# The second product of a squared-ReLU MLP by a Strassen 2x2 scheme, on one core

## Chip, core and metric

The kernel runs on one core of a Trainium2 chip. The metric is the device time of one execution in microseconds (us). TensorE does matrix products, VectorE and GpSimd elementwise work, ScalarE activations and casts, SyncE issues DMAs. In the profile they are PE (PEld is its weight load), DVE, POOL, ACT and SP.

## What is computed

One decoder block over 512 tokens with a stream of 1024 channels, in float32: a pre-norm, two token mixers side by side (latent attention and a gated convolution), a gated merge, then an MLP. Only the MLP is touched here:

```python
D_MODEL = 1024; SEQ = 512; D_FF = 4 * D_MODEL
def squared_relu_mlp(h, w_ff1, w_ff2):
    return jnp.square(jax.nn.relu(h @ w_ff1)) @ w_ff2
x = x + rms_norm(squared_relu_mlp(rms_norm(x, norm_mlp_pre), w_ff1, w_ff2), norm_mlp_post)
```

The second product is [512 x 4096] times [4096 x 1024].

## The kernel before

Float32 products are made of three matmuls on operands that are split into a rounded high half and a low half (function `mm3`, lines 86 to 88): high times high, high times low, low times high. A split is two instructions: ACT casts the source to the high half (line 91 for activations, 111 for weights), then DVE or POOL subtracts (lines 92 and 112). A matmul's moving side has up to 512 columns, its stationary side is 128 x 128.

Weights come through `wsplit` (lines 98 to 121): a 128 x 512 piece is loaded by an SP DMA into one of 6 buffers (tag `raw`), and split into one of 4 buffers each for the high (`whi`) and low (`wlo`) half.

The MLP has two stages. FF1 (lines 691 to 728) makes 32 feature blocks j of 128 features; a block is 24 matmuls, its weights in two pieces, and `ff1_end` squares the positive part into `f1[j // 2][:, j % 2, :]` (128 features x 512 tokens). Then FF2 contracts the 32 blocks. For each j two pieces of `w_ff2[j]` (128 features x 512 columns each) are loaded and split, `ff2_lhs(j)` splits the block's activations, and 4 token tiles x 2 column halves x 3 = 24 matmuls accumulate into all 8 PSUM banks (tiles `po`, one bank for 128 tokens x 512 columns). All 768 matmuls of FF2 have 512 moving columns. The low halves are made on DVE here (`eng=dve`). The last TAIL = 2 blocks are taken token tile by token tile (lines 751 to 765), so that the post-norm of one tile (`square_sums`, an ACT square with a running sum and two tiny POOL instructions, then `finish`: DVE and the store) runs beside the next tile's matmuls.

The order on each engine is set by the framework that builds the program: it takes the operations as written, may bring an operation forward on its engine while it waits for nothing there, and puts in the semaphore waits. Each engine then works strictly through its own list, SP's list of DMAs too.

Of the kernel before, what the change touches and what calls it, by code (L numbers as in the profile page):

```python
# [19 lines left out]
P = 128  # L20
# [38 lines left out]
def decoder_block(ctx: ExitStack, tc: tile.TileContext, a: dict, out: bass.AP):  # L59
# [24 lines left out]
    def mm3(o, lh, ll, rh, rl, first, last):  # L84
        """o += (lh + ll)^T (rh + rl) without the product of the two low parts (below float32's last bit)"""
        pe.matmul(o, lhsT=lh, rhs=rh, start=first, stop=False)  # L86
        pe.matmul(o, lhsT=lh, rhs=rl, start=False, stop=False)  # L87
        return pe.matmul(o, lhsT=ll, rhs=rh, start=False, stop=last)  # L88
# [10 lines left out]
    def wsplit(src, name, sizes=(512, 512), dst=None, eng=None):  # L99
        """load columns of src in pieces, split each; returns the piece (hi, lo) that holds a column range"""  # L100
# [75 lines left out]
    def rotary():  # L176
        """rotary tables: rows repeat every 32 partitions, sin carries the sign of its half"""
# [17 lines left out]
    # the tensor engine's clock rises while it works: products that nothing reads, until the first data are there  # L195
# [4 lines left out]
    # ---- first columns of W_in (latents, shared rope key), token rows; the pre-norm's scale of a token is  # L200
    # applied to its row of the product ----
    sp.dma_start(vecs, a["vecs"])
    xT = []
    with ExitStack() as s1:
# [10 lines left out]
        # squares of the stream, behind the splits that the first products wait for  # L215
# [29 lines left out]
        def latents(t):  # L245
            """norms of the latents of token tile t; shared rope key, twice"""
# [17 lines left out]
        def latents_t(t, c):  # L264
            """normalised latents to feature rows"""
# [9 lines left out]
        def token_scales():  # L275
            """rstd of the tokens, by partition and along the rows"""
# [94 lines left out]
    def rope(z, name):  # L371
        """rotary embedding of two stacked heads (rows of 64), fp32"""
# [29 lines left out]
    att, vts, sts, qks, pms, pTs = [], {}, {}, {}, {}, {}  # L402
    with ExitStack() as s3:
        r2 = open_pool(s3, "r2")

        def project_pair(pr):
            """values (token rows) and rotary queries of a pair of heads"""
# [16 lines left out]
            # hi and lo of one head stacked over the rows  # L424
# [7 lines left out]
        def project(h):  # L432
            """scaled queries and keys of a head without the rotary part, feature rows, split"""
# [112 lines left out]
    # causal depthwise convolution; running channel sum for the layer norm  # L546
# [29 lines left out]
    # layer norm over channels (partitions); sums over them through the tensor engine  # L576
# [37 lines left out]
    # pointwise projection, gated merge  # L614
# [21 lines left out]
    # output projection, post-norm, residual, MLP pre-norm  # L636
# [6 lines left out]
    def square_sums(src, name, jk=None):  # L643
        """rsqrt of the mean square of two halves, plus eps"""
# [68 lines left out]
    def ff2_lhs(j):  # L713
        fh, fl = stile(f"fh{j}", F32R), stile(f"fl{j}", F32R)
        split_psum(fh, fl, f1[j // 2][:, j % 2, :])
        return fh, fl

    for j in range(NF):
        if j == NF - 2:
            first = ff2_lhs(0)  # L720
# [9 lines left out]
    order = [tps] + [scs] * 2 + [cvtile] * 2 + [ps] * 3  # L730
    po = [[order[2 * t + hf](f"po{t}{hf}") for hf in range(2)] for t in range(NT)]
    ops = []
    for j in range(NF):
        w = wsplit(a["w_ff2"][j], f"f2{j}", eng=dve)
        fh, fl = ff2_lhs(j) if j else first
        ops.append((w, fh, fl))
        if j < NF - TAIL:
            for t in range(NT):
                sl = slice(t * P, (t + 1) * P)
                for hf in range(2):  # L740
                    mm3(po[t][hf], fh[:, sl], fl[:, sl], *w(hf * 512, 512), j == 0, False)

    def finish(t, o_, r):
# [7 lines left out]
    for t in range(NT):  # L751
        sl = slice(t * P, (t + 1) * P)
        o_ = wtile(f"o{t}")
        for hf in range(2):
# [3 lines left out]
            if hf == 0 and prev:  # L758
                finish(*prev)
# [66 lines left out]
```

## Time and profile before

| | |
|---|---|
| three runs | 842.81, 844.35, 845.77 us; median 844.35 us |
| profiled execution | span 842.8 us from the first to the last instruction |
| busy share of the span | PE 98%, PEld 81%, DVE 62%, ACT 45%, POOL 25% |
| FF1, from 496 us | 160.9 us to 656.9 us |
| FF2 | 656.9 to 835.9 us, then 6.9 us to the end |

The profile gives one execution. "Busy" counts an engine's instructions from start to end; an instruction that is held up by something the profile does not show still counts as busy, so a long record of an operation that is elsewhere short is a held one. Where two rows of one engine overlap a little, the distance from start to start is what an instruction costs in a row of them.

### The profile page before, as it was taken

Reading aid. Unit: us, or ns where it says so; the run is one execution under the profiler, and the core shown is the slowest. Engines: PE = TensorE matmul, PEld = TensorE weight load, DVE = VectorE, ACT = ScalarE, POOL = GpSimd, SP = SyncE. Lnnn points to the kernel's source line nnn. Section 1 sums busy time; section 2 is a strip of 40 time slices with the busy share of each in tenths; the row PEclk is TensorE's granted clock in tenths of the full one; section 3 lists DMA queues with packets and bytes.
Section 4 is the critical chain, followed back from the end, with each engine's and each line's share of the span. In section 5 each row is a group of like instructions: output and inputs, shape, how many; then the busy total and the mean of one; then the engine's idle time right before and its main releaser. Section 6 shows DMA issues by size and latency. Waiting matters only on the chain. (4 is left out here: it accounts for less than half of the span.)

```text
span 842.8 us, 10881 instructions
## 1 busy us (share of the span) xinstructions
PE 824.0 (98%) x3882; PEld 683.4 (81%) x3882; DVE 518.8 (62%) x838; ACT 377.0 (45%) x724; POOL 210.1 (25%) x201
## 2 busy tenths in 40 slices
PE   8989999999999999899999999999999999999996
PEld 8977888887878887687778898888888888888885
DVE  5689999999999986595554533333333333333335
ACT  7567775767572224365343333332333323332333
POOL 4244433434445446548611100000000000000001
PEclk9999999999999999899999999999999999999999
DMA  8412121222113324246440113232323232223312
GB/s 258 137 40 89 51 79 51 64 66 81 63 63 101 94 95 128 69 149 204 162 151 1 51 51 101 88 100 89 99 94 94 88 100 91 88 98 100 96 54 100
DMA packets 45126, 79.57 MB, mean 94 GB/s; under 512 B 5264, under 2 KB 10256, under 8 KB 45072
## 3 DMA queue, kind: packets, MB, share of 16 engines
q1 hardware_dynamic: 44640, 77.30, 29.0%
q0 software_dynamic: 432, 1.57, 0.5%
q8 instruction: 30, 0.49, 0.2%
q14 instruction: 24, 0.20, 0.1%
HBM read 76.76 MB, written 2.10 MB: 94 GB/s over the span
## 5 line engine op out<-in xcount | busy, mean ns | idle before, releaser
L112 DVE TENSOR_TENSOR wlo_f<-raw_f,whi_f 128x512 fp32r<-128x512 f32 x124 | 85.5, 690 | 213.3 <-ACT whi_f L111 213.1
L111 ACT CAST whi_f<-raw_f 128x512 fp32r<-128x512 f32 x124 | 76.6, 619 | 227.7 <-PE po L88 116.5
L559 DVE SCALAR_TENSOR_TENSOR cv<-u,convw,cv 128x512 f32<-128x512 f32 x232 | 161.8, 746 | 0.2
L87 PE MATMUL po<-wlo_f,fh 128*128 128x512 f32 x256 | 101.1, 395 | 0.0
L86 PE MATMUL po<-whi_f,fh 128*128 128x512 f32 x256 | 101.0, 395 | 0.0
L88 PE MATMUL po<-whi_f,fl 128*128 128x512 f32 x256 | 101.0, 395 | 0.0
L88 PE MATMUL pf<-h2h,wlo_f 128*128 128x512 f32 (+1 forms) x256 | 97.4, 381 | 0.0
L87 PE MATMUL pf<-h2l,whi_f 128*128 128x512 f32 (+1 forms) x256 | 97.4, 381 | 0.0
L86 PE MATMUL pf<-h2h,whi_f 128*128 128x512 f32 (+1 forms) x256 | 97.4, 380 | 0.0
L649 POOL TENSOR_SCALAR v_o<-ss_o 128x1 f32<-128x1 f32 x4 | 1.2, 302 | 351.5 <-ACT jo L647 351.5
L87 PEld LDWEIGHTS po<-wlo_f,fh 128*128 128x128 f32 x256 | 48.2, 188 | 11.4 <-DVE wlo_f L112 0.2
L88 PEld LDWEIGHTS po<-whi_f,fl 128*128 128x128 f32 x256 | 48.2, 188 | 11.3
L86 PEld LDWEIGHTS po<-whi_f,fh 128*128 128x128 f32 x256 | 48.2, 188 | 11.2
L112 POOL TENSOR_TENSOR wlo_gt<-raw_gt,whi_gt 128x512 fp32r<-128x512 f32 x32 | 43.9, 1374 | 50.5 <-ACT whi_gt L111 50.5
L88 PEld LDWEIGHTS pf<-h2h,wlo_f 128*128 128x128 f32 x256 | 48.2, 188 | 9.9
L87 PEld LDWEIGHTS pf<-h2l,whi_f 128*128 128x128 f32 x256 | 48.2, 188 | 9.9
L86 PEld LDWEIGHTS pf<-h2h,whi_f 128*128 128x128 f32 x256 | 48.3, 188 | 9.8
L86 PE MATMUL pg<-hTh,whi_gt 128*128 128x512 f32 x128 | 51.8, 405 | 0.0
L88 PE MATMUL pg<-hTh,wlo_gt 128*128 128x512 f32 x128 | 50.6, 395 | 0.0
L87 PE MATMUL pg<-hTl,whi_gt 128*128 128x512 f32 x128 | 50.6, 395 | 0.0
L111 ACT CAST whi_gt<-raw_gt 128x512 fp32r<-128x512 f32 x32 | 19.8, 618 | 41.3 <-PE pg L87 38.2
L86 PEld LDWEIGHTS pg<-hTh,whi_gt 128*128 128x128 f32 x128 | 24.6, 192 | 5.6 <-issue 0.5
(274 smaller groups left out, 1884.1 us busy)
## 6 DMA issues: line engine op xcount, KB each, us to landing
raw_f<-in_w_ff SPq DMA_DIRECT2D x128, 256.0 KB, 2.8
raw_gt<-in_w_zm SPq DMA_DIRECT2D x32, 256.0 KB, 2.6
raw_gb<-in_w_zm SPq DMA_DIRECT2D x16, 256.0 KB, 2.7
raw_ga<-in_w_zm SPq DMA_DIRECT2D x16, 256.0 KB, 2.6
raw_wo<-in_w_o SPq DMA_DIRECT2D x16, 256.0 KB, 2.7
raw_pw<-in_w_pw SPq DMA_DIRECT2D x16, 256.0 KB, 2.9
raw_wout<-in_w_out SPq DMA_DIRECT2D x16, 256.0 KB, 3.0
xT<-in_x_t SPq DMA_DIRECT2D x8, 256.0 KB, 4.2
```

The lines of the kernel that those rows point to most:

```text
L86: pe.matmul(o, lhsT=lh, rhs=rh, start=first, stop=False)
L87: pe.matmul(o, lhsT=lh, rhs=rl, start=False, stop=False)
L88: return pe.matmul(o, lhsT=ll, rhs=rh, start=False, stop=last)
L111: recent[act] = act.copy(hi, raw)
L112: recent[e] = e.tensor_tensor(lo, raw, f32(hi), ALU.subtract)
L559: dve.scalar_tensor_tensor(co[j] if tap == CW - 1 else acc[j], src, convw[:, i, tap:tap + 1], acc[j], ALU.mult, ALU.add)
L649: pool.tensor_scalar(v, ss[:, 0:1], ss[:, 1:2], EPS, ALU.add, ALU.add)
```

## The change

Let a pair p be the blocks 2p and 2p + 1 (NP = 16 pairs). The activations of a pair are a 2 x 2 matrix of quarters (feature block x half of the tokens), its weights one of (feature block x half of the columns), and the output one of (half of the tokens x half of the columns). The change computes the quarters of the output by a Strassen scheme with seven quarter products in place of eight. A quarter product is 2 token tiles x 3 matmuls of 512 columns. Three of the seven are made in a first sweep over the pairs (banks `ab` and `p2`), four in a second one (`ab` again and `cd`), since PSUM has 8 banks. Between the sweeps the first sums are copied out (lines 804 to 809); after the second the quarters are put together from them on DVE and POOL (lines 836 to 846), and the post-norm works from SBUF instead of PSUM.

Quarters are combined before they are split. The combinations run on POOL: in the first sweep one of weights (line 767, 128 x 512) and one of activations (line 765, 128 x 256), with two in-place updates of the activations (lines 777 and 778, 128 x 256); in the second one more update (line 784, 128 x 256) and three of weights (lines 786 to 788, 128 x 512). Splits are ACT casts (line 744) and DVE subtractions (line 745): in the first sweep four of 512 elements per partition and one of 256 for a pair, in the second one of 1024 and four of 512. Combinations of weights take buffers of tag `wlo`; the split weights lie in the 4 tiles of tag `sw`, two pairs deep; split activations take one tile of tag `h`, four pairs deep. The weights are loaded three quarters a pair in the first sweep and four in the second.

```diff
-    def ff2_lhs(j):
-        fh, fl = stile(f"fh{j}", F32R), stile(f"fl{j}", F32R)
-        split_psum(fh, fl, f1[j // 2][:, j % 2, :])
-        return fh, fl
-
     for j in range(NF):
-        if j == NF - 2:
-            first = ff2_lhs(0)
         if j < BRIDGE:
             pf, w = early[j]
             ff1_part(pf, w, SPLIT, S)
@@ -727,46 +720,136 @@
             ff1_part(pf, w, 0, S)
         ff1_end(j, pf)
     gout = gain("g_out", a["norm_mlp_post"], D)
-    order = [tps] + [scs] * 2 + [cvtile] * 2 + [ps] * 3
-    po = [[order[2 * t + hf](f"po{t}{hf}") for hf in range(2)] for t in range(NT)]
-    ops = []
-    for j in range(NF):
-        w = wsplit(a["w_ff2"][j], f"f2{j}", eng=dve)
-        fh, fl = ff2_lhs(j) if j else first
-        ops.append((w, fh, fl))
-        if j < NF - TAIL:
-            for t in range(NT):
-                sl = slice(t * P, (t + 1) * P)
-                for hf in range(2):
-                    mm3(po[t][hf], fh[:, sl], fl[:, sl], *w(hf * 512, 512), j == 0, False)
-
-    def finish(t, o_, r):
+
+
+
+    half = (slice(0, 2 * P), slice(2 * P, S))
+    NP = NF // 2
+    ab = [[scs(f"poa{t}") for t in range(2)], [cvtile(f"pob{t}") for t in range(2)]]
+    p2 = [tps("po20"), ps("po21")]
+
+    def quarter(j, hf):
+        raw = rtile(f"f2{j}{hf}")
+        sp.dma_start(raw, a["w_ff2"][j][:, hf * 512:(hf + 1) * 512])
+        return raw
+
+    def wfour(name):
+
+        return [r3.tile([P, 4, 512], F32R, tag="sw", name=f"{name}{x}", bufs=4) for x in "hl"]
+
+    def combo(name):
+        return stage.tile([P, 512], F32, tag="wlo", name=name, bufs=NSPLIT)
+
+    def split(hi, lo, src):
+        act.copy(hi, src)
+        dve.tensor_tensor(lo, src, f32(hi), ALU.subtract)
+
+    def products(bank, left, right, first, last, toks=(0, 1)):
+        for t in toks:
+            sl = slice(t * P, (t + 1) * P)
+            mm3(bank[t], left[0][:, sl], left[1][:, sl], *right, first, last)
+
+    def lhs(name):
+
+        x = hpool.tile([P, 4, S], F32R, tag="h", name=name, bufs=4)
+        return [x[:, 0:2, :], x[:, 2:4, :]]
+
+    def first_sweep(p):
+        f = f1[p]
+        raw = [quarter(2 * p, 0), quarter(2 * p, 1), quarter(2 * p + 1, 0)]
+        if p == 0:
+            w = [[stage.tile([P, 512], F32R, tag="whi", name=f"b{x}{i}", bufs=NSPLIT) for i in range(3)] for x in "hl"]
+        else:
+            w = [[x[:, i, :] for i in range(3)] for x in wfour(f"bx{p}")]
+        s1 = stile(f"s1{p}")[:, :2 * P]
+        pool.tensor_tensor(s1, f[:, 0, half[1]], f[:, 1, half[1]], ALU.add)
+        t1 = combo(f"t1{p}")
+        pool.tensor_tensor(t1, raw[1], raw[0], ALU.subtract)
+        l = lhs(f"lx{p}")
+        split(l[0][:, :, half[0]], l[1][:, :, half[0]], f[:, :, half[0]])
+        split(w[0][0], w[1][0], raw[0])
+        split(w[0][1], w[1][1], raw[2])
+        split(l[0][:, 0, half[1]], l[1][:, 0, half[1]], s1)
+        split(w[0][2], w[1][2], t1)
+        for bank, l0, i in ((ab[0], (0, 0), 0), (p2, (1, 0), 1), (ab[1], (0, 1), 2)):
+            products(bank, [x[:, l0[0], half[l0[1]]] for x in l], [x[i] for x in w], p == 0, p == NP - 1)
+
+        pool.tensor_tensor(f[:, 0, half[1]], f[:, 0, half[0]], f[:, 0, half[1]], ALU.subtract)
+        pool.tensor_tensor(f[:, 0, half[0]], s1, f[:, 0, half[0]], ALU.subtract)
+
+    def second_sweep(p):
+
+        f = f1[p]
+        raw = [quarter(2 * p + i // 2, i % 2) for i in range(4)]
+        pool.tensor_tensor(f[:, 1, half[0]], f[:, 1, half[0]], f[:, 0, half[0]], ALU.subtract)
+        t3, t2, t4 = (combo(f"t{n}{p}") for n in (3, 2, 4))
+        pool.tensor_tensor(t3, raw[3], raw[1], ALU.subtract)
+        pool.tensor_tensor(t2, t3, raw[0], ALU.add)
+        pool.tensor_tensor(t4, t2, raw[2], ALU.subtract)
+        l, w = lhs(f"ly{p}"), wfour(f"by{p}")
+        split(l[0], l[1], f)
+        for i, src in enumerate((t3, t2, raw[3], t4)):
+            split(w[0][:, i, :], w[1][:, i, :], src)
+        return l, w
+
+    def second_products(p, l, w, toks=(0, 1)):
+
+        for i, (bank, (r, c)) in enumerate(((cd[0], (0, 1)), (ab[0], (0, 0)), (ab[1], (1, 0)), (cd[1], (1, 1)))):
+            products(bank, [x[:, r, half[c]] for x in l], [x[:, i, :] for x in w], p == 0, p == NP - 1, toks)
+
+    for p in range(NP):
+        first_sweep(p)
+
+    o_ = [wtile(f"o{t}") for t in range(NT)]
+    s1, s5 = ratile("s1"), ratile("s5")
+    for t in range(2):
+        act.copy(s1[:, t, :], ab[0][t])
+        dve.tensor_tensor(o_[t][:, 0, :], p2[t], s1[:, t, :], ALU.add)
+    for t in range(2):
+        act.copy(s5[:, t, :], ab[1][t])
+    ab = [[scs(f"poe{t}") for t in range(2)], [cvtile(f"pof{t}") for t in range(2)]]
+    cd = [[ps(f"poc{t}") for t in range(2)], [tps("pod0"), ps("pod1")]]
+    for p in range(NP - TAIL):
+        second_products(p, *second_sweep(p))
+
+    def finish(t, r):
         for c, n in ((0, 512), (512, 512)) if t < NT - 1 else ((0, 512), (512, 256), (768, 256)):
             hf, c1 = divmod(c, 512)
-            piece = o_[:, hf, c1:c1 + n]
+            piece = o_[t][:, hf, c1:c1 + n]
             dve.scalar_tensor_tensor(piece, piece, r, x1[t][hf][:, c1:c1 + n], ALU.mult, ALU.add)
             sp.dma_start(out[t * P:(t + 1) * P, c:c + n], piece)
 
-    prev = None
-    for t in range(NT):
-        sl = slice(t * P, (t + 1) * P)
-        o_ = wtile(f"o{t}")
+    def post(t):
+        src = [o_[t][:, hf, :] for hf in range(2)]
+        r = square_sums(src, f"o{t}")
         for hf in range(2):
-            for j in range(NF - TAIL, NF):
-                w, fh, fl = ops[j]
-                mm3(po[t][hf], fh[:, sl], fl[:, sl], *w(hf * 512, 512), False, j == NF - 1)
-            if hf == 0 and prev:
-                finish(*prev)
-        r = square_sums(po[t], f"o{t}", wtile(f"jo{t}"))
-        for hf in range(2):
-            dve.tensor_tensor(o_[:, hf, :], po[t][hf], gout[:, hf * 512:(hf + 1) * 512], ALU.mult)
-        prev = t, o_, r
-    finish(*prev)
+            dve.tensor_tensor(src[hf], src[hf], gout[:, hf * 512:(hf + 1) * 512], ALU.mult)
+        finish(t, r)
+
+    ops = [(p, *second_sweep(p)) for p in range(NP - TAIL, NP)]
+    for t in range(2):
+        u2, u3, y = (stile(f"{n}{t}") for n in ("u2", "u3", "y"))
+        order = ((ab[0], (0, 0), 1), (ab[1], (1, 0), 2), (cd[0], (0, 1), 0), (cd[1], (1, 1), 3))
+        for n, (bank, (r, c), i) in enumerate(order):
+            for p, l, w in ops:
+                products(bank, [x[:, r, half[c]] for x in l], [x[:, i, :] for x in w], False, p == NP - 1, (t,))
+            if n == 0:
+                dve.tensor_tensor(u2, ab[0][t], s1[:, t, :], ALU.add)
+                pool.tensor_tensor(y, u2, s5[:, t, :], ALU.add)
+            elif n == 1:
+                dve.tensor_tensor(o_[t][:, 1, :], ab[1][t], y, ALU.add)
+            elif n == 2:
+                dve.tensor_tensor(u3, cd[0][t], u2, ALU.add)
+                dve.tensor_tensor(o_[t + 2][:, 1, :], cd[0][t], y, ALU.add)
+                post(t)
+            else:
+                dve.tensor_tensor(o_[t + 2][:, 0, :], u3, cd[1][t], ALU.subtract)
+                post(t + 2)
```

On POOL the combinations stand behind FF1's last norm. In the names, `t` is a combination of weights, `s` one of activations; `f_4947`, `f_5002`, `f_5070`, `f_5151` are the activations of pairs 0 to 3, `raw_f` a loaded quarter. The difference of POOL's list at that place:

```order
 L649 TENSOR_SCALAR v_x_4887<-ss_x_4882 128x1 [waits Activation_49]
 L145 TENSOR_TENSOR r_x_4889<-v_x_4887,mhalf 128x1 [waits Pool_49]
-L649 TENSOR_SCALAR v_o_7424<-ss_o_7421 128x1 [waits Activation_49]
-L145 TENSOR_TENSOR r_o_7426<-v_o_7424,mhalf 128x1 [waits Pool_49]
+L767 TENSOR_TENSOR t_6187<-raw_f_6175,raw_f_6173 128x512 [waits DMAHW5_49,DMAHW6_49,DVE_49,PE_49]
+L767 TENSOR_TENSOR t_6230<-raw_f_6222,raw_f_6220 128x512 [waits DMAHW0_49,DMAHW1_49,DVE_49,PE_49]
+L767 TENSOR_TENSOR t_6273<-raw_f_6265,raw_f_6263 128x512 [waits DMAHW3_49,DMAHW4_49,DVE_49,PE_49]
+L765 TENSOR_TENSOR s_6185<-f_4947 128x256 [waits Activation_49]
+L765 TENSOR_TENSOR s_6228<-f_5002 128x256 [waits Activation_49]
+L777 TENSOR_TENSOR f_4947<-f_4947 128x256 [waits Pool_49]
```

Before, POOL's next work after that norm was the post-norm at the kernel's end. Now three combinations of weights come first, each waiting for loads and, through its `wlo` buffer, for DVE and PE; all combinations of activations stand behind them, though they read only `f`.

In the second sweep, POOL's list holds only the three combinations of weights of each pair (the updates of line 784 have been brought forward into the first sweep). For the pair whose combinations are `t_6946` to `t_6948`:

```order
L786 TENSOR_TENSOR t_6946<-raw_f_6943,raw_f_6939 128x512 [waits DMAHW4_49,DMAHW2_49,DVE_49]
L787 TENSOR_TENSOR t_6947<-t_6946,raw_f_6937 128x512 [waits DMAHW1_49,DVE_49,Pool_49]
L788 TENSOR_TENSOR t_6948<-t_6947,raw_f_6941 128x512 [waits DMAHW3_49,DVE_49,Pool_49]
```

and DVE's list for the same pair, with the activations of a later one (`ly`):

```order
L745 TENSOR_TENSOR ly_7004<-f_5070,ly_7004 128x1024 [waits Activation_49]
L745 TENSOR_TENSOR by1l<-t_6946,by1h 128x512 [waits PE_49,Activation_49]
L745 TENSOR_TENSOR by1l<-t_6947,by1h 128x512 [waits Activation_49]
L745 TENSOR_TENSOR by1l<-raw_f_6943,by1h 128x512 [waits DMAHW4_49,Activation_49]
L745 TENSOR_TENSOR by1l<-t_6948,by1h 128x512 [waits Activation_49]
```

Every row of both lists reads two operands that lie in SBUF. Where DVE had two weight pieces and one activation block for 24 matmuls before, it now has these five rows, and POOL three beside them.

## Rows read from the trace of the kernel before

**Rows 1.** The page's busy line of PE, and its chain by line.
```profile
PE 824.0 (98%) x3882; PEld 683.4 (81%) x3882; DVE 518.8 (62%) x838; ACT 377.0 (45%) x724; POOL 210.1 (25%) x201
...
PE pf L88 7%; PE pf L86 7%; PE pf L87 7%; PE po L86 7%; PE po L88 7%; PE po L87 7%; PE pm L88 2%; PE pm L86 2%; PE pm L87 2%; PE pth L681 0%; DVE o L747 0%; DVE mgl L92 0%; ACT mgh L91 0%; POOLq L814 0%; ACT jo L647 0%
```
**Rows 2.** Busy time by stretch, FF1 then FF2: engines, granted clock, DMA share, GB/s.
```profile
496.00:656.90 160.90, 160.90 (x715) 131.37 (x715) 57.48 (x87) 49.72 (x86) 0.00 (x0) 1.00 0.29 93
656.90:835.90 179.00, 178.94 (x770) 144.61 (x768) 66.49 (x105) 56.48 (x108) 2.59 (x6) 1.00 0.28 88
```
**Rows 3.** Timeline, FF2: first ACT cast of two blocks in succession.
```profile
801.64 0.62 ACT L111 CAST whi_f<-raw_f 128x512 fp32r<-128x512 f32 x1 [3.92 <-PE po L88]
...
807.22 0.62 ACT L111 CAST whi_f<-raw_f 128x512 fp32r<-128x512 f32 x1 [3.91 <-PE po L88]
```
**Rows 4.** Timeline, end of the merge: POOL and DVE subtractions that meet.
```profile
380.80 1.74 POOL L112 TENSOR_TENSOR wlo_pw<-raw_pw,whi_pw 128x512 fp32r<-128x512 f32 x1
...
383.76 1.81 POOL L112 TENSOR_TENSOR wol<-raw_wout,woh 128x512 fp32r<-128x512 f32 x1
385.52 1.76 POOL L112 TENSOR_TENSOR wlo_pw<-raw_pw,whi_pw 128x512 fp32r<-128x512 f32 x1
387.54 1.30 POOL L112 TENSOR_TENSOR wol<-raw_wout,woh 128x512 fp32r<-128x512 f32 x1 [0.26 <-ACT woh L111]
...
384.32 1.79 DVE L112 TENSOR_TENSOR wol<-raw_wout,woh 128x512 fp32r<-128x512 f32 x1
386.04 0.68 DVE L394 TENSOR_TENSOR gB<-pg,rxs 128x512 f32<-128x512 f32 x1
```
**Rows 5.** Timeline: POOL alone, three in a row, and one of 256 columns.
```profile
392.68 3.80 POOL L112 TENSOR_TENSOR wlo_pw<-raw_pw,whi_pw 128x512 fp32r<-128x512 f32 x3
...
75.21 0.74 POOL L112 TENSOR_TENSOR wlo_head<-raw_head,whi_head 128x256 fp32r<-128x256 f32 x1 [0.45 <-ACT whi_head L111]
```
**Rows 6.** Timeline: DVE subtractions in a row: 512, 256, and 1024 elements.
```profile
426.13 0.68 DVE L92 TENSOR_TENSOR mgl<-m,mgh 128x512 fp32r<-128x512 f32 x1
426.73 0.68 DVE L112 TENSOR_TENSOR wlo_f<-raw_f,whi_f 128x512 fp32r<-128x512 f32 x1
...
58.28 0.41 DVE L92 TENSOR_TENSOR cTl<-ctb,cTh 128x256 fp32r<-128x256 f32 x1
58.62 0.55 DVE L92 TENSOR_TENSOR cTl<-cta,cTh 128x384 fp32r<-128x384 f32 x1
...
245.50 1.23 DVE L535 TENSOR_TENSOR al<-att,ah 128x1024 fp32r<-128x1024 f32 x1
```
**Rows 7.** Page, costliest groups: FF1's and FF2's casts and subtractions of weights.
```profile
L112 DVE TENSOR_TENSOR wlo_f<-raw_f,whi_f 128x512 fp32r<-128x512 f32 x124 | 85.5, 690 | 213.3 <-ACT whi_f L111 213.1
L111 ACT CAST whi_f<-raw_f 128x512 fp32r<-128x512 f32 x124 | 76.6, 619 | 227.7 <-PE po L88 116.5
```
**Rows 8.** Page, DMA issues: FF1's and FF2's weights; KB, us to landing.
```profile
raw_f<-in_w_ff SPq DMA_DIRECT2D x128, 256.0 KB, 2.8
```
**Rows 9.** Busy time by stretch near the start: PE, PEld, DVE, ACT, POOL, clock, DMA, GB/s.
```profile
20.00:24.40 4.40, 4.40 (x30) 4.40 (x29) 3.18 (x4) 4.00 (x8) 1.63 (x2) 1.00 0.95 240
```
**Rows 10.** Chain of waits at the end.
```profile
835.61 0.25 PE po L88
...
838.79 0.40 DVE o L747
```
**Rows 11.** PE's longest wait, and busy time by stretch around and after it.
```profile
PE st_var L592 <- DVE s L590: 3.0, 1, 3.0
...
334.50:341.40 6.90, 6.90 (x32) 5.73 (x31) 3.98 (x5) 4.30 (x8) 6.66 (x6) 1.00 0.31 104
341.40:348.00 6.60, 3.63 (x15) 2.98 (x14) 4.15 (x4) 1.25 (x2) 3.85 (x4) 0.72 0.35 114
348.00:354.00 6.00, 6.00 (x22) 4.81 (x21) 0.88 (x4) 0.62 (x1) 1.56 (x2) 0.74 0.00 0
```

## The prediction, made before the change was run

> **What bounds the kernel now.** I read the page's busy line and its chain first. PE is busy for 98% of the span, and the chain that ended last runs through the matmuls of FF1 (pf) and FF2 (po), six lines of about 7% each [rows 1]. The table by stretch then says what the other engines have left in the two MLP stages: PE is busy all the time at the full granted clock (1.00, that is 2.4 GHz), ACT and DVE for about a third, DMA for 28%, and POOL not at all in FF1 and for 2.6 us in FF2 [rows 2]. FF2's pace comes from the timeline: two blocks in succession start their first cast 5.58 us apart (801.64 and 807.22) [rows 3], and a block is 24 matmuls, so a matmul costs 0.2325 us from start to start, and 768 of them 178.6 us, which is FF2's 179 us. Nothing but PE bounds it.
>
> **What goes.** Seven of eight products stay: 16 pairs x (18 + 24) = 672 matmuls, 96 fewer, 156.2 us of PE. If PE stayed the bound, 22.3 us would go.
>
> **What comes, and the resource that it needs.** The question is whether POOL and DVE can feed PE: a pair has 18 x 0.2325 = 4.19 us of PE in the first sweep and 5.58 us in the second. Each alone could: POOL about 4.1 and 3.8 us, DVE about 2.7 and 3.5 us (below). But they don't run beside each other. The place to see it is the end of the merge, where both have subtractions of 128x512 with two operands in SBUF [rows 4]: POOL's 383.76 lasts until 385.57, DVE's 384.32 is held for 1.79 us and ends at 386.11, and POOL's next one (385.52) ends only at 387.28. The same POOL operation takes 1.30 us when DVE has none of its kind (387.54) and DVE's 0.68 us. So they take turns. The counter-test stands in the same rows: DVE's 386.04, whose one operand is in PSUM, takes 0.68 us in the middle of a POOL instruction. All of line 745 and of lines 765 to 788 read two operands in SBUF, so in FF2 the two engines share one turn, and their times add up.
>
> Prices. POOL: 128x512 in a row 3.80 / 3 = 1.26 us; 256 columns 0.74 us alone, 0.70 in a row (the 512 one loses 0.04 the same way) [rows 5]. DVE in a row: 512 elements 0.60 us (426.13 to 426.73), 256 0.34 (58.28 to 58.62), 1024 1.23 alone, so about 1.12 [rows 6]. Taking turns it is cheaper: POOL's starts lie 1.76 us apart (383.76 to 385.52) with one DVE subtraction in between [rows 4], which leaves 0.48 us for DVE, as the two overlap at their ends; by the same 0.12 us less, 256 and 1024 elements are 0.22 and 1.00. These are my bounds for DVE.
>
> First sweep, one pair. POOL: one of 512 and four of 256 (lines 765, 777, 778, and 784, which the order brings forward): 1.26 + 2.80 = 4.06 us. DVE: four of 512, one of 256: 2.14 to 2.74. Together 6.2 to 6.8 us against PE's 4.19. Second sweep: POOL 3 x 1.26 = 3.78, DVE 1024 and four of 512: 2.92 to 3.52; together 6.7 to 7.3 us against 5.58. For 16 pairs 206 to 226 us; I take the middle, 216, since DVE's rows sometimes follow each other and sometimes a POOL row.
>
> A rule speaks to this sum. By the Trainium skill, SBUF — State Buffer, section Who interferes with whom, DVE with two SBUF inputs and a POOL instruction that reads SBUF exclude each other, and the second is blocked for the whole of the first. Taken to the letter, with each one's duration alone (1.30, 0.74; 0.69 [rows 7], 0.41, 1.23), a pair would be 7.4 + 7.9 us and the stage 245. The trace agrees on the turns, but its 1.76 us for a pair of 1.30 and 0.69 us says that the ends overlap, so I keep 216.
>
> **Off the sum.** What is done before FF2 starts at 656.9: the order puts three weight combinations of POOL first, which wait for FF1's weight buffers, then the activations. I count those three and two activations (5.2 us), and DVE's split of four pairs' activations (2.2): -7.4 us. FF1 covers them, DVE being busy for 57 of 161 us there. POOL's work is otherwise queued behind, so its idle FF1 is hardly used.
>
> Hidden: ACT's casts, 0.62 us for 512 elements [rows 7], are five a pair, under 4 us. SP issues 112 loads of 256 KB instead of 64, 29 MB in some 215 us or 137 GB/s; the trace has 240 [rows 9]. A load lands after 2.8 us [rows 8]. In the second sweep the last quarter of the next pair can be loaded only when line 787 of this one has freed a buffer; until it lands, line 788 and one or two of DVE's turns run. Copies between the sweeps read PSUM or run on ACT. If the turns were free, these would come next: that is why I add 6 us (3%) of gaps, for the first pair, whose six halves go through four `whi` buffers with waits for PE in between, for the change of sweeps, and for loads. Ends: 0 and 18 us.
>
> The end. The last two pairs' 48 matmuls (11.2 us) go token by token; their first group needs the last pair's second combination, some 2 us before DVE's last split. So PE ends 9.2 us after that split. PE waits up to 4 us ahead of that, and after its longest wait in the trace (3.0 us) the clock was granted at 0.72 and 0.74 in the next two stretches [rows 11]: half speed (1.2 GHz) for some of it. I add 2 us, ends 0 and 3.4. From the last matmul (835.86) to the end were 6.9 us [rows 10]; a DVE subtraction of 0.69 us comes before: 7.6.
>
> **Sum**: 656.9 + 216 - 7.4 + 6 + 9.2 + 2 + 7.6 = 890.3 us of span, 47.5 above the profiled execution's 842.8. The median of the runs, 844.35, is 1.5 us above that span, so I predict 892 us.
>
> **The rivals.** (1) *The turns don't bind and PE stays the bound.* POOL's 7.84 us a pair would have to run beside DVE's; FF2 took 11.2 us for two blocks, so the change wins only if DVE adds less than about 3.1 us to POOL's, instead of 5.1 to 6.3. Then: 842.8 - 22.3 + 0.7 + some 3 us of waits in the first pair, with the median's 1.5: 826 us. For it: each engine alone has room. Against it: rows 4. 6%. (2) *The change moves POOL's work into FF1*, where POOL idles: with all four activation operations of all pairs there (16 x 2.80 = 45 us) the sum would be about 847. Against it: the order puts them behind weight combinations that wait for FF1's last blocks. 4%. (3) *PE's clock falls for good.* PE would be idle a third of the first sweep. At half speed a pair costs it 8.4 + 11.2 us, more than the turns. If a third of the stage ran so, 16 x (19.5 - 13.5) / 3 = 32 us would come on top: 924. Against it: by my estimate from the two sums the waits are one or two microseconds each, and in the rows the clock fell only behind waits of 3 us and rose again under continuous work. 12%.
>
> **Numbers.** My forecast, turns as the bound, has 78%. Its low end: 206 us of turns, one block's time (5.6 us) more done ahead, no gaps, no clock loss: 867. Its high end: 226 + 18 of gaps, 5 done ahead, 3.4 of clock: 917. That is the range. A difference under 0.3% is what these runs can't tell from none. Faster by more than that: 6% and part of rival 2, so 7%; same 2%; slower 91%.
>
> **What would show it.** In FF2, POOL records of 1.7 us and DVE records of 1 to 1.8 us, their sum of 216 us filling the stage; PE busy for about three quarters, waiting for DVE's line 745; the first sweep ending near 757, FF2's last matmul near 883. Wrong, if POOL's records stay at 1.30 and DVE's at 0.69 side by side, or if PE's granted clock stays at 0.5 over stretches of tens of us.

## The result and the profile after

The changed kernel takes 894.75 us (median of 4 runs, 892.88 to 898.99), the kernel before 843.74 us beside it: a ratio of 1.0616, 95% interval 1.0583 to 1.0648. The prediction was 892 us, slower; the range was 867 to 917. The profiled execution took 893.42 us and its span is 891.7.

The busy time by stretch, after: roughly FF1, the first sweep, the second, the end (columns as in [rows 2]). The cuts are round times; in this execution FF1's last matmul begins at 654.2, the second sweep's first one at 752.0 and its last one at 874.1.
```profile
496.00:657.00 161.00, 160.23 (x700) 130.04 (x698) 60.54 (x89) 53.80 (x95) 7.66 (x7) 1.00 0.27 94
657.00:760.00 103.00, 80.50 (x304) 58.89 (x305) 83.86 (x83) 42.53 (x79) 86.51 (x79) 0.93 0.35 118
760.00:884.00 124.00, 95.39 (x363) 67.46 (x361) 95.45 (x95) 51.46 (x84) 71.74 (x52) 0.93 0.36 126
884.00:891.70 7.70, 0.00 (x0) 0.00 (x0) 2.85 (x5) 1.33 (x4) 1.35 (x2) 0.50 0.31 112
```
Up to 657 all is much as it was in [rows 2], but for 7.66 us of POOL's work and some 3 us more of DVE's. Behind that PE is busy for 78% and 77%, as predicted (three quarters), and POOL and DVE for 58 to 84%. The chain by line, on the page, has lost FF2's matmuls and gained POOL's combinations and the loads of raw quarters (against [rows 1]):
```profile
PE pf L87 6%; PE pf L86 6%; PE pf L88 6%; DMA raw_f<-in_w_ff 6%; POOL t L787 3%; POOL t L786 2%; POOL t L788 2%; PE pm L88 2%; PE pm L86 1%; PE pm L87 1%; POOL s L765 1%; POOL f L777 1%; DVE lx L745 1%; POOL t L767 1%; DVE o L819 1%
```
What the turns look like in the first sweep, in the timeline of one pair, POOL above and DVE below:
```profile
698.97 1.75 POOL L767 TENSOR_TENSOR t<-raw_f,raw_f 128x512 f32<-128x512 f32 x1 [1.15 <-DMA raw_f<-in_w_ff]
700.69 0.92 POOL L778 TENSOR_TENSOR f<-s,f 128x256 f32<-128x256 f32 x1
...
703.97 1.07 POOL L777 TENSOR_TENSOR f<-f 128x256 f32<-128x256 f32 x1
705.01 1.74 POOL L767 TENSOR_TENSOR t<-raw_f,raw_f 128x512 f32<-128x512 f32 x1
...
699.49 1.51 DVE L745 TENSOR_TENSOR lx<-s,lx 128x256 fp32r<-128x256 f32 x1
700.93 2.37 DVE L745 TENSOR_TENSOR bx7l<-raw_f,bx7h 128x512 fp32r<-128x512 f32 x2
...
704.37 1.23 DVE L745 TENSOR_TENSOR lx<-f,lx 128x512 fp32r<-128x512 f32 x1
705.51 1.51 DVE L745 TENSOR_TENSOR lx<-s,lx 128x256 fp32r<-128x256 f32 x1
```
A pair takes 6.04 us (698.97 to 705.01; the ones beside it 5.8 to 6.4). Both engines look busy throughout, but a 256-element subtraction that takes DVE 0.41 us alone [rows 6] takes 1.51, and POOL's 1.26 us [rows 5] is 1.75: each record holds the other engine's turn. In the second sweep the same, with a wait in between:
```profile
814.37 1.30 POOL L786 TENSOR_TENSOR t<-raw_f,raw_f 128x512 f32<-128x512 f32 x1 [2.88 <-DMA raw_f<-in_w_ff]
815.75 1.28 POOL L787 TENSOR_TENSOR t<-t,raw_f 128x512 f32<-128x512 f32 x1
817.11 1.62 POOL L788 TENSOR_TENSOR t<-t,raw_f 128x512 f32<-128x512 f32 x1
821.43 1.34 POOL L786 TENSOR_TENSOR t<-raw_f,raw_f 128x512 f32<-128x512 f32 x1 [2.70 <-DMA raw_f<-in_w_ff]
...
816.35 2.92 DVE L745 TENSOR_TENSOR by9l<-t,by9h 128x512 fp32r<-128x512 f32 x2 [1.97 <-ACT by9h L744]
819.20 0.68 DVE L745 TENSOR_TENSOR by9l<-raw_f,by9h 128x512 fp32r<-128x512 f32 x1
819.80 0.68 DVE L745 TENSOR_TENSOR by9l<-t,by9h 128x512 fp32r<-128x512 f32 x1
820.41 1.21 DVE L745 TENSOR_TENSOR ly<-f,ly 128x1024 fp32r<-128x1024 f32 x1
```
POOL waits 2.70 us for a raw quarter (before 821.43), and in just that time DVE does its last two splits and ly undisturbed (819.20 to 821.62). So two explanations fit these rows: the turns fill the 7.06 us of the pair, or the loads set the pace and DVE works while POOL waits. That is what the first experiments had to tell apart.

By the steps of the prediction's sum:

| step | predicted | measured |
|---|---|---|
| FF1's end (start of its last matmul) | 656.9 | 654.2 |
| from there to DVE's last split: turns, less what is done ahead, plus gaps | 214.6 | 210.0 (864.3) |
| PE after that split, clock included | 11.2 | 10.1 |
| last matmul to the end | 7.6 | 17.3 |
| span | 890.3 | 891.7 |

FF1's end moves from one execution to the next: in e11_beforeidle (below), whose FF1 is that of the kernel before, its last matmul begins at 654.5.

### The profile page after: what moved, and what is told of

It is laid out like the page before. It is cut to its first block, busy times and chain, and to the rows that moved or that the text cites. A ratio compares the mean times of both kernels' runs of the same rounds, so it can differ in the third digit from the quotient of the medians.

```text
span 891.7 us, 11076 instructions
## 1 busy us (share of the span) xinstructions
PE 820.8 (92%) x3786; PEld 664.7 (75%) x3786; DVE 639.1 (72%) x914; ACT 420.5 (47%) x792; POOL 374.0 (42%) x331
## 4 chain that ended last, share of the span: by engine, by line
PE 25%; POOL 12%; DMA 6%; DVE 5%; issue 3%; ACT 1%; POOLq 0%; SPq 0%; DVEq 0%; ACTq 0%
PE pf L87 6%; PE pf L86 6%; PE pf L88 6%; DMA raw_f<-in_w_ff 6%; POOL t L787 3%; POOL t L786 2%; POOL t L788 2%; PE pm L88 2%; PE pm L86 1%; PE pm L87 1%; POOL s L765 1%; POOL f L777 1%; DVE lx L745 1%; POOL t L767 1%; DVE o L819 1%
## 5 line engine op out<-in xcount | busy, mean ns | idle before, releaser
L112 DVE TENSOR_TENSOR wlo_f<-raw_f,whi_f 128x512 fp32r<-128x512 f32 x60 | 41.5, 691 | 93.2 <-ACT whi_f L111 93.0
L767 POOL TENSOR_TENSOR t<-raw_f,raw_f 128x512 f32<-128x512 f32 x16 | 24.8, 1547 | 178.6 <-PE pf L88 168.1
L111 ACT CAST whi_f<-raw_f 128x512 fp32r<-128x512 f32 x60 | 37.0, 620 | 99.8 <-PE pf L87 92.3
L786 POOL TENSOR_TENSOR t<-raw_f,raw_f 128x512 f32<-128x512 f32 x16 | 22.3, 1392 | 41.2 <-DMA raw_f<-in_w_ff 36.9
L112 POOL TENSOR_TENSOR wlo_ga<-raw_ga,whi_ga 128x512 fp32r<-128x512 f32 x14 | 18.7, 1337 | 34.2 <-ACT whi_ga L111 34.2
L112 POOL TENSOR_TENSOR wlo_wo<-raw_wo,whi_wo 128x512 fp32r<-128x512 f32 x16 | 20.7, 1297 | 22.9 <-ACT whi_wo L111 20.6
L112 POOL TENSOR_TENSOR wlo_gb<-raw_gb,whi_gb 128x512 fp32r<-128x512 f32 x14 | 18.9, 1357 | 25.6 <-ACT whi_gb L111 22.1
L87 PEld LDWEIGHTS pg<-hTl,whi_gt 128*128 128x128 f32 x128 | 24.5, 191 | 5.6 <-issue 0.5
L88 PEld LDWEIGHTS pg<-hTh,wlo_gt 128*128 128x128 f32 x128 | 24.3, 190 | 5.3
```

Source lines behind the costliest of these rows:

```text
L111: recent[act] = act.copy(hi, raw)
L112: recent[e] = e.tensor_tensor(lo, raw, f32(hi), ALU.subtract)
L767: pool.tensor_tensor(t1, raw[1], raw[0], ALU.subtract)
L786: pool.tensor_tensor(t3, raw[3], raw[1], ALU.subtract)
```

## The experiments

**The combinations on DVE.** Every combination as before, on the other engine (the same edit in lines 765, 777, 778 and 784 to 788):
```diff
-        pool.tensor_tensor(t1, raw[1], raw[0], ALU.subtract)
+        dve.tensor_tensor(t1, raw[1], raw[0], ALU.subtract)
```


> All eight combination instructions of a pair (s1, t1, the three feature updates, t3, t2, t4) go from POOL to DVE; POOL has nothing of them left. Theory A (DVE and POOL take turns at SBUF, and the sum of their two times sets the pace): the same operations are cheaper on DVE, by its rows in the kernel before 0.60 us for 512 elements in a row and 0.34 for 256. A pair then costs DVE 5 x 0.60 + 5 x 0.34 = 4.7 us in the first sweep and 1.12 + 7 x 0.60 = 5.3 in the second, together 10.0 against PE's 9.8, so 16 pairs take about 160 us instead of the 207 us measured between the starts and ends of the changed kernel's stage: 840 to 855 us. DVE's records fall back to 0.6 to 0.7 us for 512 elements. Theory B (the second sweep is bound by the raw quarters, whose buffer is freed only after t2 and t3 are read): the first sweep gains 1.3 us a pair or so, the second stays at 7.1 us a pair: 865 to 880 us. Theory C (POOL's combinations don't matter, the splits on DVE are too much by themselves): within 1% of the changed kernel, 886 to 900 us.

Measured: 839.92 us (839.47 to 840.91), ratio to the kernel before 0.9949 (0.9935 to 0.9964): the same arithmetic, 55 us faster than the changed kernel, and a little faster than the kernel before. FF2 up to DVE's last split, in two stretches (columns as in [rows 2], here and below):
```profile
657.00:735.00 78.00, 77.25 (x331) 61.69 (x330) 77.62 (x158) 45.81 (x89) 0.00 (x0) 1.00 0.52 174
735.00:812.00 77.00, 76.92 (x325) 59.76 (x324) 76.99 (x121) 44.66 (x68) 0.00 (x0) 1.00 0.53 171
```
PE and DVE are both busy for 99% and more, POOL not at all. From the start of FF1's last matmul to the last split the one engine takes 157 us (655.7 to 812.7) for what took the two 210; its 512-element records are 0.69 us. Theory B's second sweep of 7.1 us a pair is gone as well, although the loads are the same, and move at 174 and 171 GB/s instead of 118 and 126.

**Weights on DVE, features on POOL.** Only lines 767 and 786 to 788 changed.


> Only the four weight combinations (t1, t3, t2, t4) go to DVE; the four feature operations on 128x256 stay on POOL. Theory A (turns, times add up): first sweep DVE 3.3 us and POOL 2.8 less what ends overlap, 5.6 to 6.1 us a pair; second sweep DVE 5.3 and POOL 0.7, 5.8 to 6.0 us a pair; 16 pairs about 185 us, 22 less than measured for the changed kernel: 862 to 878 us, between it and e1_dve. Rival D (it is the weights' chain of load, three combinations, cast and split that makes PE wait, and POOL's feature operations cost nothing): as e1_dve, 838 to 845 us.

Measured: 851.81 us, ratio 1.0088 (1.0063 to 1.0113): between the two expectations, 10 us better than A's. Where the time is:
```profile
657.00:735.00 78.00, 66.05 (x267) 49.97 (x265) 73.69 (x86) 36.52 (x72) 57.54 (x51) 0.98 0.44 140
735.00:830.00 95.00, 93.24 (x387) 74.75 (x388) 91.21 (x136) 54.74 (x85) 2.57 (x3) 0.97 0.54 166
```
POOL's feature operations no longer stand behind weight combinations that wait for loads. They run ahead and are finished in the first stretch, 51 of 64 of them after FF1, and only there PE loses time (12 us). So my sum per pair was wrong in two ways: it left a share of them in the second sweep, and some run in FF1 for nothing. Theory D falls too: the feature operations do cost, 12 us against e1_dve.

**Each half of the turns taken away.** One kernel has no low halves on DVE:
```diff
-        dve.tensor_tensor(lo, src, f32(hi), ALU.subtract)
...
-            mm3(bank[t], left[0][:, sl], left[1][:, sl], *right, first, last)
+            mm3(bank[t], left[0][:, sl], left[0][:, sl], right[0], right[0], first, last)
```


> DVE's low halves of all splits are left out (the second product uses the high halves three times, so the output isn't the reference's); POOL keeps all eight combinations, ACT its casts, PE its 672 matmuls. Theory A (turns between DVE and POOL): without DVE's 5.1 to 6.3 us a pair POOL has 7.84 us a pair at its undisturbed prices (1.26 and 0.70 us), less than PE's 9.8, so the stage is PE's: 835 to 850 us, and POOL's records for 512 elements fall from 1.4 to 1.7 us to about 1.3. Theory C (POOL is simply too slow, turns or not): POOL's records stay at 1.4 to 1.7 us, and the time near 890 us. Theory B (loads): the second sweep stays near 7 us a pair, so about 865 us.

The other has no combinations:
```diff
-        s1 = stile(f"s1{p}")[:, :2 * P]
-        pool.tensor_tensor(s1, f[:, 0, half[1]], f[:, 1, half[1]], ALU.add)
-        t1 = combo(f"t1{p}")
-        pool.tensor_tensor(t1, raw[1], raw[0], ALU.subtract)
+        s1, t1 = f[:, 0, half[1]], raw[1]
...
+        t3, t2, t4 = raw[1], raw[0], raw[2]
```


> All eight combinations are left out (single quarters and feature halves are taken in their place, so the output isn't the reference's); DVE keeps every split, PE its 672 matmuls, and the loads stay. Theory A (turns): DVE alone has 5.1 to 6.3 us a pair against PE's 9.8, so PE is the bound: 835 to 850 us, with DVE's 512-element records at 0.6 to 0.7 us. Theory B (loads): quarters are freed by DVE and ACT instead of POOL; should their landing still bind the second sweep, its pace stays near 7 us a pair and the time above 860 us. Theory C (the splits alone are too much for DVE): near 890 us.

Measured: 855.41 us (ratio 1.0131, 1.0086 to 1.0176) without low halves, and 831.73 (0.9851, 0.9826 to 0.9875) without combinations. Either one alone gives back most of the loss, so neither engine is too slow by itself: theory C falls. But the first missed its 835 to 850. POOL's records are undisturbed, and yet it waits for loads; by group, in both sweeps of e2_nolo:
```profile
L785 POOL TENSOR_TENSOR t<-raw_f,raw_f 128x512 f32<-128x512 f32 x16 | 20.6, 1285 | 38.9 <-DMA raw_f<-in_w_ff 34.9 <-ACT s L805 2.2 <-ACT ly L744 1.8
...
L766 POOL TENSOR_TENSOR t<-raw_f,raw_f 128x512 f32<-128x512 f32 x14 | 18.2, 1300 | 6.3 <-DMA raw_f<-in_w_ff 4.8 <-PE pf L88 1.5
```
(Line 785 is 786 of the changed kernel; the last columns are busy us, mean ns, idle us before.) Its pairs in the second sweep begin 6.5 us apart (first casts at 728.0 and, 15 pairs on, 825.5). Besides, PE once waited 9.6 us at the change of sweeps for ACT's copies of the banks (line 805), which stand in ACT's queue between casts of by1h and by2h that wait for POOL.

**More buffers for the raw quarters.** The changed kernel, with one of four quarters of the second sweep in other buffers:
```diff
-        raw = [quarter(2 * p + i // 2, i % 2) for i in range(4)]
+        raw = [quarter(2 * p + i // 2, i % 2, i == 2) for i in range(4)]
```
where the third argument takes a buffer of tag `whi` instead of `raw`.


> The third weight quarter of each pair of the second sweep is loaded into the four high-half buffers that the second sweep doesn't use, so that more quarters can be in flight; nothing else changes. Theory B (the second sweep is bound by the raw quarters, for which POOL waits some 2.7 us a pair): the second sweep goes from about 7.1 to 6.0 us a pair or less, the time to 875 to 882 us. Theory A (the turns are the bound, and POOL's waits for a load are DVE's turns): within 6 us of the changed kernel, 888 to 900 us.

Measured: 888.64 us (887.96 to 888.7), 6 us less than the changed kernel. POOL's waits for loads nearly end, and its records grow instead, as its group shows (busy us, mean ns, idle us before and what ended it; 2053 ns, where after the change it was 1392):
```profile
L786 POOL TENSOR_TENSOR t<-raw_f,raw_f 128x512 f32<-128x512 f32 x16 | 32.8, 2053 | 11.8 <-DMA raw_f<-in_w_ff 3.7 <-DVE by9l L745 0.6 <-DVE by10l L745 0.6
```
By stretch, DVE is busy in every microsecond of the second sweep:
```profile
760.00:857.00 97.00, 82.07 (x329) 60.63 (x327) 97.00 (x71) 47.63 (x73) 77.74 (x43) 0.99 0.41 136
```
From by4h to by15h its pairs are 6.8 us apart, within 0.1 us each (776.8 to 852.0), where the changed kernel's are 7.4 (777.8 to 859.5), in steps of 7.1 to 8.6. So the turns are worth 6.8 us a pair and the loads some 0.6 on top: theory A, with a small part of B. In the changed kernel itself the loop of loads and turns sets the second sweep's pace, close above the turns alone.

**Both together.** The same buffers without DVE's low halves.


> e2_nolo and e4_raws together: no low halves on DVE (high halves three times, so part of the products is another), and each pair's third quarter of the second sweep in the high-half buffers. In e2_nolo the second sweep's first casts lay 6.5 us a pair apart (728.0 to 825.5 for 15 pairs) although POOL's records were undisturbed (1.29 us): three of them and 2.0 to 2.7 us of waiting for a load. If that loop (t2 frees a buffer, a load fills it, the next t3 reads it) is the next bound behind the turns, more buffers bring the pair to about PE's 5.6 us, and the time to 838 to 848 us. If POOL or ACT or something else sets 6.5 us, it stays at 850 to 858 us.

Measured: 844.32 us, ratio 1.0011 (0.9995 to 1.0028). The pairs are 5.6 us apart (759.6 to 804.2 for by7h to by15h), PE's pace. So behind the turns the raw buffers are the next bound, at 6.5 us a pair, and only behind them PE; the turns hid it in the changed kernel, but for those 6 us.

**Work for POOL that nobody reads.** The kernel e5_best (below; combinations on DVE) with, per pair of the second sweep:
```diff
+        for _ in range(3):
+            pool.tensor_tensor(junk, f[:, 0, :], f[:, 1, :], ALU.subtract)
```


> e5_best, and POOL computes per pair of the second sweep three subtractions of 128x512 with two operands in SBUF whose result nobody reads (as many and as large as the three it has in the changed kernel). No engine waits for them. Theory A (DVE and POOL take turns whatever becomes of the result): POOL's 3 x 1.29 us a pair come out of DVE's time, which is full; less some overlap at the ends that is 3 to 3.9 us a pair, 48 to 62 us over 16 pairs: 872 to 888 us, with DVE's 512-element records at 1 to 2 us again. Rival C (the changed kernel was slow because PE, ACT and DVE waited for POOL's results): the time of e5_best within 3 us.

Measured: 889.09 us (888.92 to 889.25), 51.7 us more than e5_best. No engine waits for a result; the 48 operations alone bring the time back to within 6 us of the changed kernel's 894.75, at 1.08 us each. In the trace 47 of DVE's records are longer than undisturbed ones, by 49.5 us in all: about one for each of POOL's operations. While POOL works, the timeline of DVE reads:
```profile
838.09 1.75 DVE L787 TENSOR_TENSOR t<-t,raw_f 128x512 f32<-128x512 f32 x1
839.76 1.75 DVE L745 TENSOR_TENSOR by13l<-t,by13h 128x512 fp32r<-128x512 f32 x1
841.43 1.76 DVE L788 TENSOR_TENSOR t<-t,raw_f 128x512 f32<-128x512 f32 x1
843.11 1.77 DVE L745 TENSOR_TENSOR by13l<-t,by13h 128x512 fp32r<-128x512 f32 x1
844.81 0.68 DVE L745 TENSOR_TENSOR by13l<-raw_f,by13h 128x512 fp32r<-128x512 f32 x1
845.41 0.68 DVE L745 TENSOR_TENSOR by13l<-t,by13h 128x512 fp32r<-128x512 f32 x1
```
Starts are 1.67 us apart with POOL (838.09 to 843.11, three steps) and 0.60 without (844.81 to 845.41): the 1.08 us again. This shows the turns by themselves, without the combinations as a step on anyone's path.

**The same with one operand** (`pool.tensor_scalar(junk, f[:, 0, :], 2.0, None, ALU.mult)`).


> As e8_idle2, but the three unread operations of POOL a pair have one operand in SBUF (128x512 times a constant) instead of two. e8_idle2 cost 51.7 us over e5_best, 1.08 us for each of 48. If any POOL instruction that reads SBUF holds DVE's two-operand ones, these 48 cost about as much, their duration permitting: 870 to 890 us, with DVE's 512-element records stretched. If it takes two operands on POOL to hold DVE, the time is that of e5_best, 836 to 841 us, and DVE's records stay at 0.69 us beside POOL's.

Measured: 856.57 us, 19.1 more than e5_best, 0.40 us for each of 48: neither expectation. POOL did them without a break from 659.8 to 757.5, and of DVE's instructions only some were held:
```profile
700.25 0.83 DVE L777 TENSOR_TENSOR f<-f 128x256 f32<-128x256 f32 x1
701.00 0.41 DVE L765 TENSOR_TENSOR s<-f 128x256 f32<-128x256 f32 x1
...
702.28 1.09 DVE L745 TENSOR_TENSOR lx<-f,lx 128x512 fp32r<-128x512 f32 x1
```
(0.83 for 0.42, 1.09 for 0.68.) In the whole stretch 48 of DVE's records are held, nearly all by 0.41 us, 19.6 us together: one for every operation of POOL, which is the 19.1 us. So the price depends on POOL's form of instruction; why it is 0.4 us stays open, and as most of them ran in the first sweep, the two kernels aren't alike in place.

**The same in the kernel before.** Three per two blocks in its FF2, where DVE is busy for a third:
```diff
+        for _ in range(2 - j % 2):
+            pool.tensor_tensor(f1[j // 2][:, j % 2, :], f1[j // 2][:, j % 2, :], f32(fl), ALU.subtract)
```


> The kernel before, and in its FF2 POOL computes three unread subtractions of 128x512 for every two feature blocks (48 in all, as many as in e8_idle2), each between a block's low half and its features, which nothing reads afterwards. Theory A: the turns are the same as in e8_idle2, but DVE has only some 4.2 us of work in the 11.2 us of two blocks, and POOL's 3.9 us fit beside it: within 0.3% of the kernel before, 842 to 847 us, with some of DVE's records at 1.8 us. Rival: a held DVE subtraction makes its block's low half late and PE waits for it each time, half a microsecond to a microsecond for each of 48: 865 to 890 us.

Measured: 844.08 us (10 runs), ratio 0.9997 (0.9984 to 1.0011): nothing. POOL's records were held, DVE's hardly; between two blocks DVE waits 3.7 us for ACT, and POOL's turn lies there:
```profile
L738 POOL TENSOR_TENSOR f<-f,fl 128x512 f32<-128x512 f32 x45 | 69.1, 1536 | 91.6 <-DVE fl L92 90.4
...
L112 DVE TENSOR_TENSOR wlo_f<-raw_f,whi_f 128x512 fp32r<-128x512 f32 x60 | 42.4, 706 | 108.3 <-ACT whi_f L111 108.3
```
The same 48 instructions cost 52 us where DVE is full and nothing where it is not.

**The end.** Two halves of a post-norm apart, `y` on DVE; first in the changed kernel, then with the combinations on DVE:
```diff
-                pool.tensor_tensor(y, u2, s5[:, t, :], ALU.add)
+                dve.tensor_tensor(y, u2, s5[:, t, :], ALU.add)
...
-                post(t)
+                due.append(post(t))
```


> The changed kernel with the rewritten end alone (the add for y on DVE, gain, residual and store of a token tile one group of products later); the combinations stay on POOL. In the changed kernel 17.3 us passed between the last matmul and the end, where my sum had 7.6. If DVE's queue behind POOL's norms makes these ten, they go: 884 to 888 us. If they come from the turns of the last pairs, the time stays within 3 us of the changed kernel.

Measured: 900.89 us (894.36 to 903.79), no faster than the changed kernel (892.88 to 898.99), a miss. In the profiled executions the end did shrink, from 17.5 to 13.7 us behind the start of the last matmul (885.27 of 898.9), but the second sweep took 7.6 us a pair instead of 7.2 (first casts 755.8 to 870.3, against 751.4 to 859.5), with POOL waiting 45.8 us for quarters instead of 36.9. The sweeps' instructions and their order are the same in both. Why this one keeps the longer step, which the changed kernel shows now and then (7.4 to 8.6), is open; e4_raws, whose steps are all alike, suggests the load loop.


> All combinations on DVE as in e1_dve, and the end rewritten: the add for y goes to DVE, and a token tile's post-norm is cut in two, its squares at once, its gain, residual and store one group of products later, so that DVE doesn't stand behind POOL's norm with PE's next outputs queued behind it. In e1_dve PE was busy all through FF2 and its last matmul began at about 817 us, but the end came some 20 us after that. If that rest is DVE's queue (my reading), the end falls about 8 us behind the last matmul, as in the kernel before with its 6.9: 824 to 829 us, which would beat the kernel before by about 2%. Rival: PE's last products are late because DVE is busy 30 of 30 us; one more add on it and the same splits then leave the end where it was, 835 to 840 us.

Measured: 837.42 us (836.02 to 839.35), ratio to the kernel before 0.992 (0.9898 to 0.9941), the best here, 2.5 us under e1_dve where I wanted 11 to 16. Its last matmul begins at 815.16 and the span is 834.3. What fills the 19 us is plain in DVE's rows, which follow each other almost without a gap:
```profile
812.57 0.69 DVE L840 TENSOR_TENSOR u<-poe,s 128x512 f32<-128x512 f32 x1
...
824.95 1.28 DVE L827 TENSOR_TENSOR o<-o,g_out 128x512 f32<-128x512 f32 x2
826.15 1.41 DVE L819 SCALAR_TENSOR_TENSOR o<-o,r_o,x 128x512 f32<-128x512 f32 x2
827.48 1.28 DVE L827 TENSOR_TENSOR o<-o,g_out 128x512 f32<-128x512 f32 x2
829.52 1.54 DVE L819 SCALAR_TENSOR_TENSOR o<-o,r_o,x 128x512 f32<-128x512 f32 x3 [0.76 <-POOL r_o L145]
```
It isn't the order: it is DVE's own work, six sums (`y` among them), four gains and four residuals for each pair of token tiles, some 9 us, for both pairs behind the last split. In e3_nocombo, where DVE has room, the end is 17.6 us long too (last matmul 813.43, span 831.0).


> e5_best, with the gain multiplications of token tiles 1 and 2 on POOL, and tile 2's residual and store behind the last but one product of the second tiles, so that DVE doesn't stand before POOL's gain. In e5_best DVE was busy without a gap from its last split (812.6 us) to its last instruction (831.0), 18.4 us, with PE done at 815.6: 24 instructions for sums, gains and residuals. If DVE's queue is what the end consists of, four of 0.60 us less and the order give 3 to 4 us: 833 to 835 us. If POOL's gains (1.3 us each, in turns with DVE's residuals) hold DVE up instead, the time stays at 836 to 840 us.

Measured: 839.84 us, ratio 0.9953 (0.9939 to 0.9966), no better. The turns are back: with POOL's gains beside them, two of DVE's residuals are held (2.42 us for two instead of 1.41, 1.74 for one instead of 0.75), and one waits for POOL's norm behind a gain.
```profile
818.91 2.42 DVE L819 SCALAR_TENSOR_TENSOR o<-o,r_o,x 128x512 f32<-128x512 f32 x2
...
823.00 1.74 DVE L819 SCALAR_TENSOR_TENSOR o<-o,r_o,x 128x512 f32<-128x512 f32 x1 [1.07 <-POOL r_o L145]
```

## Why the prediction was right

- **The bound.** "In FF2 the two engines share one turn, and their times add up" holds, and it is shown from three sides: take either engine's share away (831.73, 855.41), give all to one (839.92), or add unread work to the other (889.09). The argument rested on five rows of another stage [rows 4]. Of the signs that I named, the first sweep shows the records of 1 to 1.8 us; in the second POOL's are mostly 1.3 to 1.6 and three of DVE's five a pair are undisturbed, since both wait within a pair for a load and a cast. Both sweeps ended 7 to 9 us before the times that I gave (749.8 for 757, 874.4 for 883).
- **The turns, 216 us.** Some 5 too high. In the 210.0 us of the stage at least one of POOL and DVE is in an instruction of line 745 or lines 765 to 788 for 204.1 us; with what was done ahead (7.1, below) that is 211 us of turns. Where both have work all the time a pair is cheaper: 6.04 us in the first sweep and 6.8 in the second without the load loop (e4_raws), 205 us for 16 of both, the low end of my range. The term that was mis-sized is DVE's share of a turn: I had bounds of 0.48 to 0.60 us and took the middle, but in e8_idle2 a pair of turns is 1.67 us, which leaves 0.41 beside POOL's 1.26. That the stage cost more than 205 fits stretches in which one engine works alone and no ends overlap. The rule of the Trainium skill that I weighed (SBUF — State Buffer, Who interferes with whom: the second is blocked for the whole of the first) is right about who holds whom where both have two operands. By the letter its 245 us would have been 34 too many, since the ends overlap; and in e9_idle1 the 0.41 us held are far from the whole of POOL's instruction.
- **Done ahead, and gaps.** Both came out as summed: by 654.2 POOL had done 4.9 us and DVE 2.2 (7.1, forecast 7.4), and for 5.9 us of the stage neither was at work (forecast 6). The loads alone, which I had put into the gaps, cost some 6 us (e4_raws). PE's longest wait, 7.1 us in the first sweep for bx5h, is no gap of the turns: POOL is busy for 12.92 of the 13 us from 677 to 690, mostly with feature operations that stand before the next weight combination (685.53) in its list, and bx5's quarter is loaded only behind that. It isn't there when the weights' combinations are on DVE (e_wdve's longest wait is 2.5).
- **PE after the last split**: 10.1 us against 11.2. The clock did fall to half behind the long waits, as allowed for (granted 0.50 from 861.5 to 867.1, behind a wait of 4.6 us; 0.93 in both sweeps' stretches), and cost little as the turns were the bound; rival 3 did not come.
- **The end, 7.6 us, was 17.3: the step that failed.** I added one subtraction of 0.69 us to the end of the kernel before [rows 10]. But each group of products now completes two token tiles at once, and DVE has 13 operations of 128x512 for them (five sums, four gains, four residuals), in which a tile's norm on POOL holds the next tile's sums:
```profile
874.12 0.40 PE L88 MATMUL pod<-by15h,ly 128*128 128x512 f32 x1
...
877.57 1.42 DVE L819 SCALAR_TENSOR_TENSOR o<-o,r_o,x 128x512 f32<-128x512 f32 x2 [2.06 <-POOL r_o L145]
878.90 0.68 DVE L840 TENSOR_TENSOR o<-pof,y 128x512 f32<-128x512 f32 x1
...
886.92 1.54 DVE L819 SCALAR_TENSOR_TENSOR o<-o,r_o,x 128x512 f32<-128x512 f32 x3 [0.84 <-POOL r_o L145]
```
  PE is done at 874.4, and DVE still has the last two tiles' sums before it. I should have counted DVE's instructions behind the last matmul, as I did for the sweeps.
- So that the total is off by only 0.3% is luck: the stage was put 4.6 us too high, PE's rest 1.1, FF1's end happened to lie 2.7 us earlier, and the end, 10 us too low, cancels them. (By their own terms the ends of my range are 868 and 918, not 867 and 917; nothing hangs on it.)
- **Rival 1** (PE as the bound, 826 us) did not come. In e1_dve PE is full in both sweeps all the same, since the turns are gone with POOL's work; that it takes 839.92 us and not 826 is the end, 23 us behind its last matmul (815.28 of 838.4). Rival 2 (POOL's work moved into FF1) was not tried on its own; e_wdve shows it in small.

## What to carry to other kernels

Two engines that share a turn are one resource: add their times for the same stretch before giving one of them the other's work, and ask first which of the two does the operation in less time; here DVE alone (0.60 us each) beat DVE and POOL together (1.67 for two). A held instruction costs nothing where the holder's victim has slack: the same 48 instructions cost 0 us in one FF2 and 52 in the other. And when a change alters what is finished last, count every engine's instructions behind the last matmul, not only the ones that were added.

## What the runs showed of the hardware

- Two subtractions of 128x512, one on POOL and one on DVE, both with two operands in SBUF, take 1.67 us for the two in steady alternation, while alone they take 1.26 and 0.60 in a row: their ends overlap by some 0.2 us.
- A POOL operation with one SBUF operand and a constant held one DVE instruction for 0.41 us, not for its own length (1.5 to 2.4 us in its records, the first one apart), and cost 0.40 us each instead of 1.08.
- The second sweep's loop of loads and turns settled at 7.3 us a pair in the changed kernel (808.5 to 852.1 for six) and at 7.8 in e6_tail (800.2 to 862.8 for eight), with the same instructions in the same order.
- The turn does not always alternate: in e8_idle2 one POOL subtraction that could start at 739.36 stands for 25.31 us, another (810.76) for 13.99, while DVE's rows follow each other undisturbed, 0.60 us apart for 512 elements; the alternation sets in only then. What lets POOL in at last isn't shown.
